# A two-layer diffusion trunk on one core: the first parameter loads regrouped, a weight strip cut differently, one rounding step moved between engines, and a new planned order

## The chip, the core and the metric

The kernel runs on one NeuronCore of a Trainium2 chip. Its engines are TensorE (PE in the profile, its weight loads PEld), VectorE (DVE), ScalarE (ACT), GpSimd (POOL) and SyncE (SP), which issues most DMAs; ScalarE can issue DMAs as well (ACTq). The metric is the time of one execution in microseconds (us) of device time; lower is better.

## The reference

Two layers work on 256 latent tokens and 256 context tokens, each of 1024 numbers in float32. A layer computes six modulation vectors from a conditioning vector, `silu(c) @ w_mod + b_mod`, normalises and modulates the tokens, multiplies them by an input matrix of 1024 x 3096, runs three groups of mixing heads on the result, multiplies by an output matrix, and adds that to the tokens. A mixture of 32 experts (each token takes two) follows. In short:

```python
mod = split(silu(c) @ w_mod[l] + b_mod[l], 6)
h   = (rmsnorm(x, norm1_w[l]) * (1 + mod[1]) + mod[0]) @ w_in[l]      # 3096 columns
m   = concat(diff_attention(h), ssm_mixer(h), gdn_mixer(h))          # three head groups
x   = x + mod[2] * (m @ w_out[l])
x   = x + mod[5] * hier_moe(modulate(rmsnorm(x, norm2_w[l]), mod[3], mod[4]))
```

In the 3096 columns of `w_in`, columns 2048 to 2055 are `dt`, the eight step sizes of the state-space heads; columns 2056 to 2311 are `q`, 2312 to 2567 `k` and 2568 to 2823 `v` of the delta-rule heads; columns 2824 to 3095 are that group's gate with 16 rate columns.

## The kernel before

The program is written as a list of operations (`Prog.record`), which a planner then puts in order (`Prog._schedule`). The planner keeps a clock for each engine and takes, again and again, the operation that could start first; among equals the one of highest priority. A priority is the cost of what still hangs on an operation, plus a bias by label (`CFG`, such as `"inQ"` or `"OUT2"`), plus random noise of a given size and seed (`ORDER`: one tuple of run length, noise, seed and warm gap for each of three parts of the program). Each engine executes its own list strictly in the planned order. SP's DMAs keep the order in which the code names them. Where the planner expects TensorE to be idle for longer than the warm gap it fills the gap with idle products (L536). All memory is one arena that the planner hands out; loaded weights share a ring of limited size, so a load can wait until an older weight has been used.

The planner's costs are a model. A mark with `after=n` keeps the operations under it from being planned before the first n of the list (DMAs of SP aside) are all planned.

The beginning of layer 0, the stretch that the diff touches, works so:

- SP loads `c`, constants, the four token tiles (512 KB each, `xtok`), then `wm0`, the eight 1 MB chunks of `w_mod` that give the first two modulation vectors (L971), then the first four strips of `w_in` (`first_loads`, L1063), and so on.
- ScalarE's queue issues 28 small parameter loads (the list `small`, L953 to L973): row vectors of both layers into the tiles `ra`, `row` and `rb`. After `csil` it also issues the two loads `wdt` (L984): eight columns of `w_in` for each layer, 1024 runs of 32 bytes each.
- TensorE transposes the token tiles; ScalarE and VectorE copy them out to `xT`; ScalarE squares them (L1005), `inverse` makes the reciprocal norm, and VectorE makes the products `v0` (L1009), eight of 128x512.
- `modulation` (L874) multiplies the eight `w_mod` chunks and adds `b_mod`; `mod_cols` makes the columns of scale and shift.
- For each of eight feature blocks k (L1099 on), `h` is wanted in two parts: `hhi`, rounded to float32r, and `hlo`, the remainder. With `v0`, ScalarE writes `hhi` directly (two ACTIVATEs of 128x256), VectorE makes the same value unrounded as `u` (two TENSOR_SCALARs of 128x256), and VectorE (even k) or GpSimd (odd k) subtracts.
- `tokm(0, ...)` (L1218) is the first projection: strip 0 (272 columns) and `wdt` (8 columns) are split into a rounded part and a remainder by `split` (L1046), and each of four token tiles takes 24 products of 280 columns. Its results start the chain "rates". Then `feat` projects k (strip 1), v (strip 2) and q (strip 3).
- `param_prep` (L1015) turns the small parameters into columns and broadcasts; it is the first thing recorded after the token part, ahead of `mixers`.

Later stretches, which only the new order touches: the rest of layer 0's mixers, to about 560 us; layer 0's experts; layer 1's mixers; layer 1's experts.

Of the kernel before, what the change touches and what calls it, by code (L numbers as in the profile page):

```python
# [9 lines left out]
F32 = mybir.dt.float32  # L10
# [102 lines left out]
TICK, WARM = 3413.3, 2800.0  # L113
# [661 lines left out]
def trunk(tc, pg, A, out, xd, dbg, layers, stop):  # L775
# [43 lines left out]
    def transpose(o, i):  # L819
        pe.transpose(o, i, ident[:i.shape[0], :i.shape[0]])  # L820
# [47 lines left out]
    ra = [T([104, P], name="ra") for _ in range(2)]  # L868
# [82 lines left out]
    wdt = T([P, 2, KC, 8], name="wdt", stays=True)  # L951
    gp.memset(row, 0.0)
    small = []  # L953
    for l in range(2):
        small += [(ra[l][0:48, :], A["b_mod"][l].rearrange("(r p) -> r p", p=P)),
                  (ra[l][48:56, :], A["norm1_w"][l].rearrange("(r p) -> r p", p=P)),
                  (ra[l][56:64, :], A["norm2_w"][l].rearrange("(r p) -> r p", p=P)),
                  (ra[l][64:70, :], A["ssm_conv_b"][l].rearrange("(r p) -> r p", p=P)),
                  (ra[l][70:100, :], A["ssm_conv_w"][l].rearrange("t (i p) -> (t i) p", p=P)),
                  (ra[l][100:104, :], A["ssm_norm_w"][l].rearrange("(r p) -> r p", p=P))]  # L960
    for o, nm, n in ((0, "ssm_dt_bias", 16), (16, "gdn_dt_bias", 8), (32, "ssm_a_log", 16), (48, "gdn_a_log", 8),
                     (56, "ssm_d", 8), (64, "router_g_b", 4), (68, "router_e_b", 32), (104, "diff_lq1", 32),
                     (136, "diff_lq2", 32), (168, "diff_lk1", 32), (200, "diff_lk2", 32)):
        ap = A[nm]
        small.append((row[:, :, o:o + n], bass.AP(tensor=ap.tensor, offset=ap.offset, ap=[[0, 1], [n, 2], [1, n]])))
    small.append((rb[0:60, :], A["gdn_conv_w"].rearrange("l t (i p) -> (l t i) p", p=P)))
    for o, nm, n in ((60, "diff_norm_w", 64), (62, "gdn_norm_w", 64), (64, "diff_qn_w", 32), (66, "diff_kn_w", 32)):
        ap = A[nm]
        small.append((rb[o:o + 2, :].rearrange("p (h q) -> p h q", q=n),
                      bass.AP(tensor=ap.tensor, offset=ap.offset, ap=[[n, 2], [0, P // n], [1, n]])))  # L970
    wm0 = [mod_load(l0, 0, k) for k in range(KC)]  # L971
    for dst, src in small:
        ac.dma_start(dst, src)  # L973
# [8 lines left out]
                     cs.rearrange("p (s k) -> p s k", s=2), OP.mult)  # L982
    for l in range(2):
        ac.dma_start(wdt[:, l], A["w_in"][l].rearrange("(k p) n -> p k n", p=P)[:, :, 2048:2056], wait=[csil])  # L984

    def row_prep(l):
        pt = ps("pt")
        transpose(pt[:, 0:104], ra[l])
        ve.tensor_copy(prm[l][:, 0:64], pt[:, 0:64])
        ve.tensor_scalar(prm[l][:, 64:104], pt[:, 64:104], 0.5, None, OP.mult)  # L990

    row_prep(0)
# [22 lines left out]
    def param_prep():  # L1015
        ve.tensor_copy(identb, ident)
        for n_, nm in zip(negm, ("le", "ge")):
            ve.tensor_scalar(n_, c(nm), 1.0, 1e30, OP.subtract, OP.mult)
        row_prep(1)
        o = ps("pbc")  # L1020
        mm(o[:, 0:464], c("ones")[0:1].to_broadcast([1, P]), row.rearrange("p l x -> p (l x)"))
        ve.tensor_copy(bcs.rearrange("p l x -> p (l x)"), o[:, 0:464])
        pt = ps("pt")
        transpose(pt[:, 0:68], rb)
        ve.tensor_scalar(pb[:, 0:60], pt[:, 0:60], 0.5, None, OP.mult)
        ve.tensor_copy(pb[:, 66:68], pt[:, 66:68])
        ve.tensor_scalar(pb[:, 62:64], pt[:, 62:64], 0.5, None, OP.mult)
        ve.tensor_scalar(pb[:, 64:66], pt[:, 64:66], 32 ** -0.5, None, OP.mult)
        for l in range(2):
            li = 0.8 - 0.6 * math.exp(-0.3 * l)  # L1030
            ve.tensor_scalar(pb[:, 60 + l:61 + l], pt[:, 60 + l:61 + l], 1.0 - li, None, OP.mult)
# [31 lines left out]
    def first_loads(l):  # L1063
# [3 lines left out]
        pieces += [W[:, :, a:a + 256] for a in (2312, 2568, 2056,  # L1067
# [5 lines left out]
        for i, p_ in enumerate(pieces[:4]):  # L1073
            ws.append(wload(p_, 8, 256 if i else 272, "w"))
            if i == 1 and l == layers[0]:
                cast_consts()
        return pieces, ws, {(1, 0): split(ws[1], 0, P, CFG[l]["parts"])} if CFG[l]["early"] else {}


    def mixers(l, wm=None, v0=None):  # L1080
# [18 lines left out]
        for k in range(KC):  # L1099
            u = T([P, TOK], name="hk")  # L1100
            for s in range(2):
                sl = slice(256 * s, 256 * s + 256)
                sc, bi = cols(s, k)
                if v0:
                    ac.activation(hhi[k][:, sl], v0[k][:, sl], AF.Identity, scale=sc, bias=bi)
                    ve.tensor_scalar(u[:, sl], v0[k][:, sl], sc, bi, OP.mult, OP.add)
# [7 lines left out]
            if k % 2 and not v0:  # L1114
                ac.copy(hhi[k], u)
            if k % 2 or v0:
                (gp if k % 2 else ve).tensor_tensor(hlo[k], u, hhi[k].bitcast(F32), OP.subtract)
# [67 lines left out]

        pieces, ws, early = first_loads(l)
        WZ, WS = 7, 9
# [30 lines left out]
        tokm(0, 272, 256, got, wdt[:, l])  # L1218
# [102 lines left out]
        for i in range(2):  # L1321
            o = feat(1, P * i)
# [5 lines left out]
        for i in range(2):  # L1328
            o = feat(2, P * i)
# [3 lines left out]
        for i in range(2):  # L1333
            o = feat(3, P * i, lo)
# [815 lines left out]
    mark("params")  # L2150
    param_prep()
    for l in layers:
# [13 lines left out]
ORDER = [(2500.0, 1500.0, 994, 900.0), (2500.0, 100.0, 270, 600.0), (0.0, 500.0, 79, 2000.0)]  # L2166
# [3 lines left out]
    {"rings": 26624, "ring0": 6, "gdn": 5e+05, "inS": 0, "inZ": 1e+05, "SSM": 1e+05, "inQ": 4.29e+05, "inV": 2e+05,  # L2170
     "ATT": 1e+05, "mod": 0, "OUT": 47800, "OUT2": 50000, "route": 1e+05, "ring": 2.5, "units": 3, "proj": 2, "gate":
     1, "lssm": 2, "latt": 3, "early": 1, "ahead": 11, "loop": 0, "nowait": -1, "mroute": 0, "mpos": 14, "modr":
     1e+06, "parts": 2, "margin": (8, 16, 0)},
    {"rings": 28672, "ring0": 6, "gdn": 1e+06, "inS": 7.15e+05, "inZ": 2e+06, "SSM": 50000, "inQ": 50000, "inV":
     12400, "ATT": 1e+06, "mod": 0, "OUT": 50000, "OUT2": 0, "route": 4e+06, "ring": 2, "units": 3, "proj": 4, "gate":
     1, "lssm": 2, "latt": 2, "early": 1, "ahead": 9, "loop": 0, "nowait": -1, "mroute": 3, "mpos": 9, "modr": 6e+05,
     "parts": 2, "margin": (16, 8, 1)}]
# [23 lines left out]
```

## Time and profile before

| what | value |
|---|---|
| median of 3 runs | 1909.54 us (1909.12 to 1909.98) |
| the profiled execution, its own time | 1907.57 us |
| its span in the profile | 1905.8 us |
| busy share of PE, DVE, ACT, POOL | 93%, 47%, 28%, 21% |
| mean granted TensorE clock | 0.971 of full speed |
| moved by DMA | 503.41 MB, 264 GB/s over the span |

The span runs from the first to the last instruction; 1.8 us of the execution's own time lie around it. Busy shares are averages over stages with different limits. A granted clock of 1.00 is 2.4 GHz and of 0.50 is 1.2 GHz; a stretch between them is a mixture in time. In a row that ends in `[1.36 <-DVE arena_r L352]`, the engine sat idle for 1.36 us before that instruction and VectorE ended the wait. Nearly every instruction carries line L352, that of the helper that records it, so shapes tell the rows apart.

### The profile page before, as it was taken

Reading aid. Unit: us, or ns where it says so; the run is one execution under the profiler, and the core shown is the slowest. Engines: PE = TensorE matmul, PEld = TensorE weight load, DVE = VectorE, ACT = ScalarE, POOL = GpSimd, SP = SyncE. Lnnn points to the kernel's source line nnn. Section 1 sums busy time; section 2 is a strip of 40 time slices with the busy share of each in tenths; the row PEclk is TensorE's granted clock in tenths of the full one; section 3 lists DMA queues with packets and bytes.
Section 4 is the critical chain, followed back from the end, with each engine's and each line's share of the span. In section 5 each row is a group of like instructions: output and inputs, shape, how many; then the busy total and the mean of one; then the engine's idle time right before and its main releaser. Section 6 shows DMA issues by size and latency. Waiting matters only on the chain. (4 is left out here: it accounts for less than half of the span.)

```text
span 1905.8 us, 34790 instructions
## 1 busy us (share of the span) xinstructions
PE 1781.1 (93%) x13912; PEld 1266.5 (66%) x13912; DVE 891.4 (47%) x2440; ACT 542.6 (28%) x1432; POOL 403.4 (21%) x649
## 2 busy tenths in 40 slices
PE   5889999989989999999999999999899999999998
PEld 2767786657975656657565878877686655566654
DVE  3785556855531433333234885766751323222222
ACT  2466444533310101111011466564321111011101
POOL 0254453474100000000000346652910000000000
PEclk8898989998989999999999999999899999999999
DMA  8510006373159999899999520106929999999997
GB/s 301 196 45 26 21 2 220 113 263 128 63 196 371 421 420 421 334 390 421 376 422 385 172 79 20 46 24 243 339 93 361 421 420 421 421 421 420 421 421 289
DMA packets 108272, 503.41 MB, mean 264 GB/s; under 512 B 14893, under 2 KB 39753, under 8 KB 53833
## 3 DMA queue, kind: packets, MB, share of 16 engines
q1 hardware_dynamic: 105552, 500.91, 66.5%
q8 instruction: 112, 1.84, 0.4%
q10 hardware_dynamic: 2553, 0.21, 0.1%
q14 instruction: 55, 0.45, 0.1%
HBM read 495.85 MB, written 5.24 MB: 263 GB/s over the span
## 5 line engine op out<-in xcount | busy, mean ns | idle before, releaser
L352 PE MATMUL psum<-arena 128*64 128x256 f32 (+14 forms) x9808 | 1190.4, 369 | 99.0 <-DVE arena L352 38.2
L352 PEld LDWEIGHTS psum<-arena 128*64 128x64 f32 (+3 forms) x9784 | 734.2, 147 | 521.5 <-issue 219.0
L352 PE MATMUL psum<-arena_r 128*128 128x256 f32 (+3 forms) x3336 | 604.2, 330 | 20.7 <-ACT arena_r L352 6.5
L352 PEld LDWEIGHTS psum<-arena_r 128*128 128x128 f32 x3336 | 486.4, 195 | 107.1 <-issue 36.7
L352 POOL TENSOR_TENSOR arena<-arena 128x128 f32<-128x128 f32 (+4 forms) x500 | 272.5, 568 | 275.9 <-DVE arena L352 142.9
L352 DVE SCALAR_TENSOR_TENSOR arena<-psum,arena 128x256 f32<-128x256 f32 (+4 forms) x649 | 271.3, 473 | 94.8 <-PE psum L352 81.1
L352 ACT COPY arena<-psum 64x128 f32<-64x128 f32 (+3 forms) x524 | 176.9, 358 | 458.0 <-PE psum L352 371.2
L352 DVE SCALAR_TENSOR_TENSOR arena<-arena,psum 128x256 f32<-128x256 f32 (+1 forms) x194 | 84.6, 442 | 407.9 <-PE psum L352 208.2
L352 POOL TENSOR_TENSOR arena_r<-arena,arena_r 128x512 fp32r<-128x512 f32 (+3 forms) x55 | 78.1, 1426 | 639.9 <-PE psum L352 500.7
L352 DVE TENSOR_TENSOR arena<-arena,psum 64x128 f32<-64x128 f32 (+4 forms) x384 | 116.3, 320 | 116.1 <-PE psum L352 65.5
L352 ACT ACTIVATE arena<-psum 128x256 f32<-128x256 f32 (+2 forms) x103 | 37.3, 366 | 360.6 <-PE psum L352 347.0
L352 DVE SCALAR_TENSOR_TENSOR arena_r<-psum,arena,arena_r 128x512 fp32r<-128x512 f32 x64 | 47.5, 748 | 175.0 <-ACT arena_r L352 174.5
L352 ACT ACTIVATE arena<-arena 128x256 f32<-128x256 f32 (+8 forms) x204 | 85.2, 445 | 138.3 <-DVE arena L352 107.5
L352 ACT ACTIVATE arena_r<-psum,arena 128x512 fp32r<-128x512 f32 x64 | 43.9, 687 | 247.7 <-PE psum L352 247.5
L352 ACT ACTIVATE arena<-psum,arena 128x128 f32<-128x128 f32 (+2 forms) x216 | 88.2, 464 | 75.7 <-PE psum L352 58.9
L352 DVE COPY arena<-psum 128x512 f32<-128x512 f32 (+10 forms) x117 | 39.8, 350 | 125.9 <-PE psum L352 113.7
L352 ACT CAST arena_r<-arena 128x512 fp32r<-128x512 f32 (+3 forms) x140 | 83.3, 635 | 41.4 <-PE psum L352 27.0
L352 DVE TENSOR_TENSOR arena_r<-arena,arena_r 128x512 fp32r<-128x512 f32 (+4 forms) x93 | 80.1, 877 | 21.1 <-ACT arena_r L352 20.3
L352 DVE SCALAR_TENSOR_TENSOR arena<-arena 128x4 f32<-128x4 f32 (+6 forms) x264 | 78.0, 308 | 10.9 <-POOL arena L352 5.5
L352 DVE TENSOR_TENSOR arena<-arena 128x4 f32<-128x4 f32 (+9 forms) x234 | 75.3, 341 | 10.1 <-ACT arena L352 6.9
L352 DVE TENSOR_SCALAR arena<-arena 128x4 int32<-128x4 int32 (+16 forms) x162 | 45.6, 301 | 14.7 <-DMA arena<-in_consts_dram 8.6
L536 PE MATMUL psum<-arena 128*128 128x128 f32 x384 | 49.0, 283 | 0.0
(31 smaller groups left out, 306.0 us busy)
## 6 DMA issues: line engine op xcount, KB each, us to landing
arena<-in_exp_w_gate_dram SPq DMA_DIRECT2D x128, 1024.0 KB, 19.8
arena<-in_exp_w_up_dram SPq DMA_DIRECT2D x128, 1024.0 KB, 12.5
arena<-in_exp_w_down_dram SPq DMA_DIRECT2D x120, 1024.0 KB, 17.0
arena<-in_w_mod_dram SPq DMA_DIRECT2D x48, 1024.0 KB, 5.3
arena<-in_w_in_dram SPq DMA_DIRECT2D x22, 1024.0 KB, 9.4
arena<-in_exp_w_down_dram SPq DMA_DIRECT2D x16, 512.0 KB, 17.2
xd<-arena SPq DMA_DIRECT2D x16, 256.0 KB, 4.7
arena<-xd SPq DMA_DIRECT2D x16, 256.0 KB, 5.3
```

What stands on the lines that cost most here:

```text
L352: inst(*[self.real(a) for a in args], **{k: self.real(a) for k, a in kw.items()})
L536: self.nc.tensor.matmul(o, one, one, start=True, stop=True, skip_group_check=True)
```

## The change

It has five parts.

1. The early parameter loads on ScalarE's queue shrink from 28 to three (`b_mod`, `norm1_w`, `norm2_w`, each for both layers at once). The others, 20 loads now, go to SP's queue as `small_loads`, named after strip 1 of `w_in` and ahead of strip 2.
2. `wdt` is gone. `dt` and q come in one strip of 264 columns, loaded as the second strip; k and v follow as third and fourth. The first projection takes its `dt` from that strip, and q is projected from its columns 8 on.
3. `prm` is filled in two steps: the modulation's columns early, the rest in `param_prep`, which is now recorded within `mixers` under a mark with `after=n0`, so that it is planned once all of `h` is.
4. In the first norm, ScalarE writes `u` (float32), VectorE copies it to `hhi` and makes all eight subtractions; GpSimd makes none there.
5. `ORDER` and `CFG` have other values, and the planner counts TensorE as warm from 3000 instead of 2800 on.

```diff
-TICK, WARM = 3413.3, 2800.0
+TICK, WARM = 3413.3, 3000.0
...
-    for l in range(2):
-        small += [(ra[l][0:48, :], A["b_mod"][l].rearrange("(r p) -> r p", p=P)),
...
-    for dst, src in small:
-        ac.dma_start(dst, src)
+    for r0, r1, ap in ((0, 48, A["b_mod"].rearrange("l (r p) -> r l p", p=P)),
+                       (48, 56, A["norm1_w"].rearrange("l (r p) -> r l p", p=P)),
+                       (56, 64, A["norm2_w"].rearrange("l (r p) -> r l p", p=P))):
+        ac.dma_start(ra[r0:r1], ap)
     wm0 = [mod_load(l0, 0, k) for k in range(KC)]
+    def small_loads():
+        for r0, r1, ap in ((64, 70, A["ssm_conv_b"].rearrange("l (r p) -> r l p", p=P)),
+                           (100, 104, A["ssm_norm_w"].rearrange("l (r p) -> r l p", p=P))):
+            sy.dma_start(ra[r0:r1], ap)
+        for l in range(2):
+            sy.dma_start(ra[70:100, l, :], A["ssm_conv_w"][l].rearrange("t (i p) -> (t i) p", p=P))
+        for o, nm, n in ((0, "ssm_dt_bias", 16), (16, "gdn_dt_bias", 8), (32, "ssm_a_log", 16), (48, "gdn_a_log", 8),
+                         (56, "ssm_d", 8), (64, "router_g_b", 4), (68, "router_e_b", 32), (104, "diff_lq1", 32),
+                         (136, "diff_lq2", 32), (168, "diff_lk1", 32), (200, "diff_lk2", 32)):
+            ap = A[nm]
+            sy.dma_start(row[:, :, o:o + n], bass.AP(tensor=ap.tensor, offset=ap.offset, ap=[[0, 1], [n, 2], [1, n]]))
+        sy.dma_start(rb[0:60, :], A["gdn_conv_w"].rearrange("l t (i p) -> (l t i) p", p=P))
+        for o, nm, n in ((60, "diff_norm_w", 64), (62, "gdn_norm_w", 64), (64, "diff_qn_w", 32), (66, "diff_kn_w", 32)):
+            ap = A[nm]
+            sy.dma_start(rb[o:o + 2, :].rearrange("p (h q) -> p h q", q=n),
+                         bass.AP(tensor=ap.tensor, offset=ap.offset, ap=[[n, 2], [0, P // n], [1, n]]))
...
-        ac.dma_start(wdt[:, l], A["w_in"][l].rearrange("(k p) n -> p k n", p=P)[:, :, 2048:2056], wait=[csil])
...
         pieces = [W[:, :, 2824:3096]]
-        pieces += [W[:, :, a:a + 256] for a in (2312, 2568, 2056,
+        pieces += [W[:, :, 2048:2312]]
+        pieces += [W[:, :, a:a + 256] for a in (2312, 2568,
...
             if i == 1 and l == layers[0]:
+                small_loads()
+            if i == 2 and l == layers[0]:
                 cast_consts()
...
                 if v0:
-                    ac.activation(hhi[k][:, sl], v0[k][:, sl], AF.Identity, scale=sc, bias=bi)
-                    ve.tensor_scalar(u[:, sl], v0[k][:, sl], sc, bi, OP.mult, OP.add)
+                    ac.activation(u[:, sl], v0[k][:, sl], AF.Identity, scale=sc, bias=bi)
...
-            if k % 2 and not v0:
-                ac.copy(hhi[k], u)
             if k % 2 or v0:
-                (gp if k % 2 else ve).tensor_tensor(hlo[k], u, hhi[k].bitcast(F32), OP.subtract)
+                (ve.tensor_copy if v0 else ac.copy)(hhi[k], u)
+                (ve if v0 else gp).tensor_tensor(hlo[k], u, hhi[k].bitcast(F32), OP.subtract)
...
+        n0 = len(pg.ops)
         pieces, ws, early = first_loads(l)
+        if v0:
+            mark("params", after=n0)
+            param_prep()
+            mark("norm")
...
-        tokm(0, 272, 256, got, wdt[:, l])
+        tokm(0, 272, 256, got, ws[1][:, :, 0:8])
...
-            o = feat(3, P * i, lo)
+            o = feat(1, 8 + P * i, lo)
...
-ORDER = [(2500.0, 1500.0, 994, 900.0), (2500.0, 100.0, 270, 600.0), (0.0, 500.0, 79, 2000.0)]
+ORDER = [(2500.0, 1500.0, 298, 2000.0), (2500.0, 100.0, 42, 900.0), (0.0, 1000.0, 754, 900.0)]
```

In `CFG` of layer 0, `inZ` goes from 1e5 to 1.79e5, `inQ` from 4.29e5 to 1e6, `inV` from 2e5 to 1e5, `ATT` from 1e5 to 1.1e5, `mod` from 0 to 4540, `OUT` from 47800 to 50200, and `nowait` from -1 to 0 (strip 0 may now be split before `hhi[0]` is there). In that of layer 1, `inQ` goes from 50000 to 42800, `inV` from 12400 to 16700, `OUT2` from 0 to 1e6 and `route` from 4e6 to 1.86e7.

## Rows read from the trace of the kernel before

**Rows 1.** Busy time by windows: us, engines' busy time, clock, DMA share, GB/s.
```profile
core 0: us, PE busy (x) PEld busy (x) DVE busy (x) ACT busy (x) POOL busy (x), PEclk, DMA share, GB/s
0.00:10.00 10.00, 2.13 (x9) 1.66 (x10) 0.94 (x6) 1.47 (x2) 0.91 (x6) 1.00 0.64 191
...
17.50:20.00 2.50, 2.38 (x21) 0.69 (x13) 1.49 (x8) 0.87 (x4) 0.44 (x3) 1.00 0.16 26
...
25.00:27.50 2.50, 1.79 (x9) 0.49 (x2) 0.00 (x0) 0.00 (x0) 0.00 (x0) 0.50 1.02 424
27.50:30.00 2.50, 2.50 (x10) 0.35 (x12) 1.22 (x6) 0.28 (x2) 0.35 (x3) 0.50 0.63 182
30.00:32.50 2.50, 1.88 (x12) 0.20 (x4) 0.95 (x6) 1.15 (x4) 0.00 (x0) 0.72 0.69 197
...
42.50:45.00 2.50, 0.94 (x9) 0.70 (x7) 1.96 (x7) 0.48 (x2) 0.00 (x0) 1.00 1.12 361
```

**Rows 2.** Waits of SP's own queue, first 60 us: total, times, longest.
```profile
SPq L352 <- DMA arena<-in_w_in_dram: 21.6, 4, 9.8
```

**Rows 3.** Timeline of SP and ACT: start, length, what, [idle before].
```profile
7.92 23.04 SPq L352 DMA_DIRECT2D arena<-in_w_mod_dram  x8
...
9.64 0.41 ACTq L352 DMA_DIRECT2D arena<-in_w_in_dram  x1
...
15.28 0.57 ACTq L352 DMA_DIRECT2D arena<-in_gdn_a_log_dram  x1
...
21.74 0.45 ACTq L352 DMA_DIRECT2D arena<-in_w_in_dram  x1
...
31.92 1.06 ACT L352 ACTIVATE arena<-arena 128x1024 f32<-128x1024 f32 x1 [1.07 <-PE psum L352]
...
44.60 1.09 ACT L352 ACTIVATE arena_r<-arena 128x256 fp32r<-128x256 f32 x2 [2.02 <-DVE arena L352]
```

**Rows 4.** Timeline of PE and DVE, 40 to 74 us.
```profile
40.12 3.31 PE L352 MATMUL psum<-arena 128*32 128x512 f32 x20 [0.44 <-DMA arena<-in_w_mod_dram]
...
46.85 0.40 PE L352 MATMUL psum<-arena_r 128*128 128x280 f32 x1 [3.41 <-ACT arena_r L352]
...
65.61 8.80 PE L352 MATMUL psum<-arena_r 128*128 128x280 f32 x57 [1.36 <-DVE arena_r L352]
...
72.70 0.18 DVE L352 COPY arena<-psum 128x24 f32<-128x24 f32 x1
```

**Rows 5.** Groups by shape, DVE, 40 to 66 us: busy us, mean ns, idle.
```profile
L352 DVE TENSOR_TENSOR arena_r<-arena,arena_r 128x512 fp32r<-128x512 f32 x6 | 7.7, 1304 | 0.0
L352 DVE TENSOR_SCALAR arena<-arena 128x256 f32<-128x256 f32 x16 | 6.8, 468 | 0.9 <-POOL arena_r L352 0.7
L352 DVE TENSOR_TENSOR arena<-arena,psum 128x512 f32<-128x512 f32 x8 | 5.4, 681 | 2.8 <-PE psum L352 2.6
L352 DVE TENSOR_TENSOR arena_r<-arena,arena_r 128x1088 fp32r<-128x1088 f32 x1 | 1.3, 1278 | 0.0
L352 DVE CAST arena<-arena 128x1024 bf16<-128x1024 f32 x1 | 0.7, 676 | 0.0
```

**Rows 6.** Groups by shape, ACT, 40 to 66 us.
```profile
L352 ACT ACTIVATE arena_r<-arena 128x256 fp32r<-128x256 f32 x16 | 8.4, 591 | 8.2 <-DVE arena L352 8.2
L352 ACT CAST arena_r<-arena 128x1088 fp32r<-128x1088 f32 x2 | 2.2, 1088 | 0.0
```

**Rows 7.** Groups by shape, PE, 46 to 74 us.
```profile
L352 PE MATMUL psum<-arena_r 128*128 128x280 f32 x96 | 15.4, 317 | 9.9 <-DVE arena_r L352 4.1 <-ACT arena_r L352 3.4 <-POOL arena_r L352 2.3
```

**Rows 8.** Busy time by windows, the later stages.
```profile
100.00:150.00 50.00, 46.63 (x421) 35.96 (x419) 40.76 (x109) 30.69 (x88) 23.12 (x35) 1.00 0.13 43
...
80.00:600.00 520.00, 481.13 (x3978) 380.48 (x3978) 305.63 (x920) 222.56 (x640) 205.07 (x345) 0.93 0.34 120
600.00:1050.00 450.00, 439.25 (x3195) 278.83 (x3191) 161.16 (x377) 49.31 (x102) 0.48 (x1) 1.00 0.98 399
```

**Rows 9.** Idle products (L536) alone, 80 to 600 us.
```profile
80.00:600.00 520.00, 7.83 (x60) 7.17 (x60) 0.93 0.34 120
```

More of the change, by code (lines that the diff above doesn't have):

```diff
@@ L867, in trunk @@
     csil = T([P, KC, 32], name="csil", stays=True)
-    ra = [T([104, P], name="ra") for _ in range(2)]
+    ra = T([104, 2, P], name="ra")
     prm = [T([P, 104], name=f"prm{l}", stays=True) for l in range(2)]
@@ L950, in trunk @@
     row = T([1, 2, 232], name="row")
-    wdt = T([P, 2, KC, 8], name="wdt", stays=True)
     gp.memset(row, 0.0)
-    small = []
-    for l in range(2):
-        small += [(ra[l][0:48, :], A["b_mod"][l].rearrange("(r p) -> r p", p=P)),
[L956 to L970, printed above, removed]
-    wm0 = [mod_load(l0, 0, k) for k in range(KC)]
-    for dst, src in small:
-        ac.dma_start(dst, src)
+    for r0, r1, ap in ((0, 48, A["b_mod"].rearrange("l (r p) -> r l p", p=P)),
+                       (48, 56, A["norm1_w"].rearrange("l (r p) -> r l p", p=P)),
+                       (56, 64, A["norm2_w"].rearrange("l (r p) -> r l p", p=P))):
+        ac.dma_start(ra[r0:r1], ap)
@@ L982, in trunk @@
                      cs.rearrange("p (s k) -> p s k", s=2), OP.mult)
+    pt = ps("pt")
     for l in range(2):
-        ac.dma_start(wdt[:, l], A["w_in"][l].rearrange("(k p) n -> p k n", p=P)[:, :, 2048:2056], wait=[csil])
[L986 to L992, printed above, removed]
+        transpose(pt[:, 64 * l:64 * l + 64], ra[0:64, l, :])
+        ve.tensor_copy(prm[l][:, 0:64], pt[:, 64 * l:64 * l + 64])
     xx = T([P, KC, TOK], name="xT")
@@ L1018, in param_prep @@
             ve.tensor_scalar(n_, c(nm), 1.0, 1e30, OP.subtract, OP.mult)
-        row_prep(1)
+        for l in range(2):
+            pt = ps("pt")
+            transpose(pt[:, 0:104], ra[:, l, :])
+            ve.tensor_scalar(prm[l][:, 64:104], pt[:, 64:104], 0.5, None, OP.mult)
         o = ps("pbc")
@@ L1073, in first_loads @@
         for i, p_ in enumerate(pieces[:4]):
-            ws.append(wload(p_, 8, 256 if i else 272, "w"))
+            ws.append(wload(p_, 8, (272, 264, 256, 256)[i], "w"))
             if i == 1 and l == layers[0]:
+                small_loads()
+            if i == 2 and l == layers[0]:
                 cast_consts()
-        return pieces, ws, {(1, 0): split(ws[1], 0, P, CFG[l]["parts"])} if CFG[l]["early"] else {}
+        return pieces, ws, {(2, 0): split(ws[2], 0, P, CFG[l]["parts"])} if CFG[l]["early"] else {}
     def mixers(l, wm=None, v0=None):
@@ L1321, in mixers @@
         for i in range(2):
-            o = feat(1, P * i)
+            o = feat(2, P * i)
             conv(o, gk[i], gw(2 + i), 0.0)
@@ L1328, in mixers @@
         for i in range(2):
-            o = feat(2, P * i)
+            o = feat(3, P * i)
             vt = T([P, TOK], name="cv")
@@ L2148, in output @@
                 sy.dma_start(out[0, P * t:P * t + P, 512 * h:512 * h + 512], y)
-    mark("params")
-    param_prep()
     for l in layers:
@@ L2169 @@
 CFG = [
[L2170 to L2177, printed above, removed]
+    {"rings": 26624, "ring0": 6, "gdn": 5e+05, "inS": 0, "inZ": 1.79e+05, "SSM": 1e+05, "inQ": 1e+06, "inV": 1e+05,
+     "ATT": 1.1e+05, "mod": 4540, "OUT": 50200, "OUT2": 50000, "route": 1e+05, "ring": 2.5, "units": 3, "proj": 2,
+     "gate": 1, "lssm": 2, "latt": 3, "early": 1, "ahead": 11, "loop": 0, "nowait": 0, "mroute": 0, "mpos": 14,
+     "modr": 1e+06, "parts": 2, "margin": (8, 16, 0)},
+    {"rings": 28672, "ring0": 6, "gdn": 1e+06, "inS": 7.15e+05, "inZ": 2e+06, "SSM": 50000, "inQ": 42800, "inV":
+     16700, "ATT": 1e+06, "mod": 0, "OUT": 50000, "OUT2": 1e+06, "route": 1.86e+07, "ring": 2, "units": 3, "proj": 4,
+     "gate": 1, "lssm": 2, "latt": 2, "early": 1, "ahead": 9, "loop": 0, "nowait": -1, "mroute": 3, "mpos": 9, "modr":
+     6e+05, "parts": 2, "margin": (16, 8, 1)}]
 _INS = ['x', 'c', 'ctx', 'c_ctx', 'w_mod', 'b_mod', 'norm1_w', 'norm2_w', 'w_in', 'w_out', 'diff_qn_w', 'diff_kn_w',
```

## The prediction

> **What bounds the kernel now.** I read the windows first. From 600 to 1050 us, the first experts, DMA is busy 0.98 at 399 GB/s and PE 439 of 450 us: weights stream at full rate and PE barely keeps up. From 80 to 600 us PE is busy 481 of 520 us while DMA is busy 0.34, and 0.13 from 100 to 150 us [rows 8]. So the mixers are bound by PE and what it waits for, and the experts by their stream, which waits for memory that the mixers free. Neither has a date of its own: if the mixers begin earlier, the rest moves along. The last layer is built the same.
>
> The beginning is different. In its first 70 us neither holds. The rows to see: DMA moves 26 GB/s at 17.5 to 20 us, 182 and 197 GB/s at 27.5 to 32.5 us, against 424 GB/s just before the second hole [rows 1]. SP is at that time handing out the `w_mod` chunks, from 7.92 to 30.96 us [rows 3]. What it waited for is the `w_in` loads, 21.6 us in four waits, the longest 9.8 us [rows 2]; before 31 us the only `w_in` loads are the two `wdt`, issued on ScalarE's queue at 9.64 and 21.74 us [rows 3]. A wait of SP's queue for a load of ScalarE's queue, with no data between the two, is what leaves the DMA engines empty. The last `w_mod` chunk is used at 40.12 us [rows 4], the first modulated block starts at 44.60 us [rows 3], TensorE's last wait for `hlo` or a split strip ends at 65.61 us, and the last result of the first projection is copied out at 72.70 us [rows 4]. These four times are the scale for what follows.
>
> **The change part by part.**
>
> *Early loads and `wdt`.* Until the last `w_mod` chunk, DMA must move 0.43 MB of constants, 2.1 MB of tokens and 8.39 MB of `w_mod`, by the shapes 10.9 MB. With no holes, at 424 GB/s [rows 1], that is 25.7 us; the first 10 us moved only 1.9 MB [rows 1]. If they go as before, the other 9.0 MB end at 31.2 us; if the rate is full from 2.5 us on, at 28.2 us. I take 30 us for the use of the last chunk, against 40.12: **10 us earlier**. From the other side: the holes alone, 2.5 us at 26 and 5 us at 190 instead of 424 GB/s, are worth 2.3 + 2.8 = 5.1 us. From there to the first modulated block I leave the 4.5 us of before (40.12 to 44.60): 34.5 us.
>
> ScalarE loses some 25 DMA issues, up to 0.57 us each [rows 3], and the waits among them. Its four squares, which began at 31.92 us [rows 3] although the tokens had landed long before, can run by 20 us, and so the eight products `v0` on DVE, 5.4 us [rows 5], which lay between the blocks of `h`, come before the modulation.
>
> *The tokens.* On ScalarE nothing changes in number: 16 ACTIVATEs, 8.4 us, and 2.2 us for strip 0's casts [rows 6], with the narrower strips some 12 us. On DVE the 16 TENSOR_SCALARs (6.8 us) go. Eight copies of 128x512 come: the trace has none of this form; half of the 1024-wide CAST is 0.34 us, a two-input operation of that width 0.68 us [rows 5]; I take 0.4, since it too has one input, 3.2 us in all. Four more subtractions come from GpSimd, so eight at 0.68 us are 5.4 us; before, six of that kind had a mean of 1.30 us [rows 5]. With strip 0's share of 1.3 us and small ones DVE has some 10 us, at most 13. DVE and ScalarE work side by side: `h` and the split strip take some 13 us after the first block instead of 21.0 (44.60 to 65.61): ready at 47.5, **18 us earlier**.
>
> *Strip with `dt`.* The first product now needs strips 0 and 1, 2.2 MB, at 361 GB/s 6 us [rows 1]: 36 us, before most of `h`. The first projection's 96 products take 15.4 us of PE [rows 7]; PE was at half clock in part of that time before, when it stood waiting for `h` [rows 1, 7]. Starting at 37 us and with 3 us for a slow clock at the start it ends at 56 us, now bound by PE itself, against 72.70: **16 us earlier**. Bounds: 53 us with no slow clock (20 us), 62 us if it can start only at 46 (10 us). The 128-word `wdt` tile and its two splits become a view of strip 1: nothing either way. In layer 1 `dt` is likewise in the second strip, loaded ahead in the shadow of the last experts; I price that at 0, and at up to 3 us, one strip's transfer, if that cover is gone. Strip 1 stays in the ring until q is projected, which holds back loads used tens of us later: 0.
>
> *The 20 loads on SP.* One such load took 0.57 us to issue on ScalarE's queue [rows 3]; the eleven into `row` at that, and the nine others at half of it by estimate, take 9 us of SP's time. Behind them stand strip 2 (k), the constants, strip 3 (v) and the stores of `xT`. Strip 2 then lands at about 36 + 9 + 3 = 48 us; PE wants it when the first projection ends, 56 us. Covered by 8 us; without cover at most 9 us. Behind the parameters wait `param_prep`'s operations on PE and DVE, but the mark puts them after the last block of `h`, at 47.5 us, when the last loads land: 0 to 3 us, which the 3 us for PE's slow start may hide.
>
> The Trainium skill (DMA: Bandwidth & Descriptors, Issuing engines are not separate DMA queues) says that DMAs of several engines share the same 16 DMA engines, and that issuing from several saves only the sequencers' issue time. By it, moving 20 loads onto SP buys nothing and gives back that saving; taken strictly it would also make ScalarE's loads nearly free to SP before, and the trace disagrees, with 9.8 us of one wait.
>
> *The new order.* It moves every later stage by an amount that no row gives. What it can win or lose lies between 80 and 600 us: PE idles 520 - 481 = 39 us there, and a mean clock of 0.93 is worth 0.07 x 520 = 36 us [rows 8]. A new drawing of noise and biases I put at 0, give or take 8 us, about a tenth of the two together. The wider warm gap drops some of the 60 idle products [rows 9], too few to matter.
>
> Sum: 1907.57 us (the profiled execution's own time) less 16 is 1891.6; that execution lies 2.0 us under the median, so **1893.5 us**.
>
> **The rivals.**
>
> *SP's queue becomes the brake* (12 in 100). If the 20 issues hold the parameters and strip 2 back beyond 50 us, or planned operations on PE queue up behind the parameters ahead of the first projection, that projection starts at 46 and ends at 62 us: 10 us won, 1899.5. For it: TensorE and DVE execute in planned order, and the planner reckons each SP issue at 50 ns. Against it: the mark `after=n0`. It is the case that the Trainium skill's rule on issuing engines (DMA: Bandwidth & Descriptors) points to.
>
> *The order is better as well* (10 in 100): half-clock and idle time between 80 and 600 us falls by a tenth to a fifth more, 12 us: 1881.
>
> *The gain stays at the beginning* (7 in 100): later stages wait for something with a date of its own, and the end does not move: 1908. Against it speaks DMA's idleness from 100 us on [rows 8].
>
> *Slower* (11 in 100): the new order with its wide warm gap leaves gaps in which the clock falls. It decides once the loss to half clock grows from 36 to over 52 us, 16 more. If it grows by two thirds, 24 us, the time is 1917. Against it: only 7.8 us of idle products stood between 80 and 600 us [rows 9], so little was held up by them.
>
> **How the numbers follow.** The forecast has 60 in 100, with its own range of 1885 to 1902: 16 us with bounds of 10 and 20, and 8 for the order, not all of them at once. Measurements of this kernel tell 0.2%, 3.8 us, from no change. Faster: 60 + 12 + 10 and 2 of the third rival, 84 in 100; same 5; slower 11. The range for 8 in 10 reaches from 1881, the better order, to 1908, where the gain is lost, and leaves out the slower case and half of the better one.
>
> **What would show it.** In the profile after: no hole in DMA before 36 us; SP's waits for `w_in` gone; the last `w_mod` chunk used at about 30 us; the first modulated block at 34 to 35, the first projection's end at 53 to 58 us; GpSimd without subtractions for `h`; at 600 us and at the end the same distance of some 16 us. I am wrong in the sum if the distance at 75 us is under 8 us; wrong about the passage if it is 16 there and gone at 1050 us; wrong about the order if it changes by over 8 us between 80 and 600 us.

## The result: 1890.6 us, 1.0% less, and the time forecast came out for partly other reasons

The changed kernel takes 1890.62 us (median of 6 runs, 1886.13 to 1898.01) beside 1909.76 us for the kernel before (6 runs, 1908.64 to 1916.01): a ratio of 0.9899, 95% interval 0.9876 to 0.9923. The forecast was 1893.5 us, with a range of 1881 to 1908. The profiled execution took 1890.12 us, its span 1888.3 us.

I read the same views as before, in the same order. First the windows of the beginning of the changed kernel (columns as in [rows 1]):

```profile
17.50:20.00 2.50, 1.27 (x9) 0.29 (x9) 0.23 (x1) 2.40 (x6) 0.00 (x0) 0.98 1.01 419
...
25.00:27.50 2.50, 2.50 (x16) 1.58 (x15) 0.76 (x2) 0.00 (x0) 0.00 (x0) 0.66 1.01 419
27.50:30.00 2.50, 1.28 (x12) 0.16 (x8) 2.50 (x5) 0.00 (x0) 0.00 (x0) 1.00 1.00 397
...
37.50:40.00 2.50, 0.91 (x2) 0.66 (x3) 2.43 (x5) 1.81 (x4) 0.90 (x1) 0.50 0.00 0
40.00:42.50 2.50, 2.50 (x12) 2.50 (x12) 2.33 (x5) 1.09 (x2) 0.00 (x0) 0.50 0.00 0
42.50:45.00 2.50, 2.22 (x13) 1.99 (x11) 0.40 (x1) 0.00 (x0) 0.00 (x0) 0.75 0.05 14
```

The holes of [rows 1] are gone: 419 GB/s where 26 stood, 397 where 182 stood. A new hole has come, from 37.5 to 45 us, in which DMA moves next to nothing. The waits of SP's own queue in the first 60 us (total, times, longest) agree with the first half; 21.6 us of [rows 2] have become 5.6. Before 31 us, while SP hands out the `w_mod` chunks, its waits for `w_in` go from 18.7 us in two to none. The 5.6 us all come after that, where the kernel before waited for 2.9:

```profile
SPq L352 <- DMA arena<-in_w_in_dram: 5.6, 4, 2.4
```

The timeline of SP and ScalarE shows what lies in the new hole:

```profile
3.89 6.76 SPq L352 DMA_DIRECT2D arena<-in_w_mod_dram  x8
...
16.43 1.06 ACT L352 ACTIVATE arena<-arena 128x1024 f32<-128x1024 f32 x1 [0.32 <-PE psum L352]
...
26.77 3.56 SPq L352 DMA_DIRECT2D arena<-in_ssm_conv_b_dram  x1
...
35.74 1.73 ACT L352 ACTIVATE arena<-arena 128x256 f32<-128x256 f32 x3
...
40.62 1.09 ACT L352 ACTIVATE arena<-arena 128x256 f32<-128x256 f32 x2 [1.08 <-DVE arena_r L352]
...
43.86 0.26 SPq L352 DMA_DIRECT2D arena<-in_diff_kn_w_dram  x1
...
44.24 0.40 SPq L352 DMA_DIRECT2D arena<-in_w_in_dram  x1
...
49.70 1.14 ACT L352 CAST arena_r<-arena 128x512 fp32r<-128x512 f32 x2 [7.99 <-DMA arena<-in_w_in_dram]
50.74 4.05 ACT L352 ACTIVATE arena<-arena 128x256 f32<-128x256 f32 x8
```

The `w_mod` chunks are handed out in 6.76 us (before 23.04, [rows 3]), the squares begin at 16.43 us (31.92) and the first modulated block at 35.74 us (44.60). But from 26.77 to 44.12 us SP hands out the 20 small loads, and strip 2 goes out only behind them, at 44.24 us. ScalarE's planned list has the split of strip 2, the two CASTs, in the middle of `h`, after eight of its 16 ACTIVATEs. ScalarE stands for 7.99 us until strip 2 has landed, and the other eight ACTIVATEs come behind it. On PE and DVE (timeline, as in [rows 4]) this looks so:

```profile
31.74 1.06 PE L352 MATMUL psum<-arena 128*32 128x512 f32 x8 [2.94 <-DMA arena<-in_w_mod_dram]
...
38.83 0.57 PE L352 MATMUL psum<-arena_r 128*128 128x280 f32 x1 [4.21 <-DVE arena_r L352]
...
50.87 1.29 DVE L352 TENSOR_TENSOR arena_r<-arena,arena_r 128x512 fp32r<-128x512 f32 x2 [7.97 <-DMA arena<-in_consts_dram]
...
52.55 0.83 PE L352 MATMUL psum<-arena_r 128*128 128x280 f32 x2 [7.84 <-DVE arena_r L352]
...
68.64 0.18 DVE L352 COPY arena<-psum 128x24 f32<-128x24 f32 x1
```

The last `w_mod` chunk is used at 31.74 us instead of 40.12, the first product of the first projection comes at 38.83 instead of 46.85, and then PE and DVE stand 8 us, too. (DVE's row is its part of the split, which needs ScalarE's CASTs; the view names the constants as releaser, since they land at about the same time. An experiment below tells the two apart.) The last copy comes at 68.64 instead of 72.70 us: 4.1 us earlier, where I had forecast 16.

The prices of the moved work, by groups (DVE from 35 to 58 us, ScalarE from 10 to 60 us, PE from 0 to 70 us), answer to [rows 5 to 7]:

```profile
L352 DVE TENSOR_TENSOR arena_r<-arena,arena_r 128x512 fp32r<-128x512 f32 x10 | 6.7, 687 | 8.1 <-DMA arena<-in_consts_dram 8.0
L352 DVE CAST arena_r<-arena 128x512 fp32r<-128x512 f32 x8 | 4.7, 593 | 1.8 <-ACT arena L352 1.7
...
L352 ACT ACTIVATE arena<-arena 128x256 f32<-128x256 f32 x16 | 8.5, 594 | 1.2 <-DVE arena_r L352 1.1
...
L352 PE MATMUL psum<-arena_r 128*128 128x280 f32 x96 | 17.5, 349 | 12.7 <-DVE arena_r L352 12.7
```

And the windows of the later stages, which answer to [rows 8], with two stretches more:

```profile
0.00:600.00 600.00, 538.02 (x4309) 414.97 (x4310) 351.10 (x1038) 251.60 (x710) 212.00 (x360) 0.94 0.42 153
...
80.00:600.00 520.00, 485.91 (x4035) 377.52 (x4035) 314.48 (x942) 222.57 (x648) 205.04 (x347) 0.95 0.37 136
600.00:1050.00 450.00, 443.75 (x3233) 294.43 (x3232) 176.80 (x422) 55.09 (x113) 3.41 (x4) 0.99 0.97 393
...
600.00:640.00 40.00, 39.55 (x269) 23.14 (x269) 19.85 (x48) 4.44 (x10) 0.00 (x0) 1.00 1.01 421
```

A lead is how much earlier the changed kernel comes to the same point than the kernel before. By 600 us DMA has moved 600 x 153 GB/s = 91.8 MB. The same window of the kernel before reads 141 GB/s, 84.6 MB. From there on the experts' weights stream at full rate, 421 GB/s, so 7.2 MB more by 600 us are, by this estimate, 17 us of lead. Measured so, the lead is made in two pieces, 4 us at 70 us and another 13 between there and 600 us, and is 17.5 us at the end (1905.8 to 1888.3 us of span). At points of the program it grows and shrinks: 9.3 us where the first overflow loop of the experts is entered, the loop for experts with more tokens than their places hold (546.2 to 536.9), 25.2 at the first product of layer 1 (1074.2 to 1049.1), 18.3 where the second overflow loop is entered (1426.5 to 1408.3).

### The profile page after: what moved, and what is told of

The parts are those of the page before. It is cut to its first block, busy times and chain, and to the rows that moved or that the text cites. A ratio compares the mean times of both kernels' runs of the same rounds, so it can differ in the third digit from the quotient of the medians.

```text
span 1888.3 us, 34616 instructions
## 1 busy us (share of the span) xinstructions
PE 1766.9 (94%) x13852; PEld 1253.8 (66%) x13852; DVE 899.3 (48%) x2436; ACT 542.5 (29%) x1432; POOL 397.3 (21%) x645
## 3 DMA queue, kind: packets, MB, share of 16 engines
q8 instruction: 111, 1.82, 0.4%
## 5 line engine op out<-in xcount | busy, mean ns | idle before, releaser
L352 PE MATMUL psum<-arena 128*64 128x256 f32 (+12 forms) x9810 | 1184.2, 367 | 95.8 <-DVE arena L352 33.4
L352 PE MATMUL psum<-arena_r 128*128 128x256 f32 (+3 forms) x3336 | 594.4, 329 | 20.0 <-DVE arena_r L352 15.5
L352 POOL TENSOR_TENSOR arena<-arena 128x128 f32<-128x128 f32 (+5 forms) x500 | 275.0, 575 | 281.5 <-DVE arena L352 196.6
L352 POOL TENSOR_TENSOR arena_r<-arena,arena_r 128x512 fp32r<-128x512 f32 (+3 forms) x51 | 71.1, 1401 | 640.4 <-ACT arena_r L352 633.2
L352 ACT ACTIVATE arena<-arena 128x256 f32<-128x256 f32 (+7 forms) x220 | 92.6, 457 | 131.0 <-DVE arena L352 94.9
L352 DVE COPY arena<-psum 128x512 f32<-128x512 f32 (+12 forms) x117 | 40.3, 350 | 120.2 <-PE psum L352 99.6
L352 DVE TENSOR_TENSOR arena_r<-arena,arena_r 128x512 fp32r<-128x512 f32 (+3 forms) x97 | 85.3, 897 | 25.0 <-ACT arena_r L352 16.6
L352 DVE TENSOR_TENSOR arena<-arena 128x4 f32<-128x4 f32 (+7 forms) x234 | 76.6, 341 | 17.9 <-ACT arena L352 14.8
L352 DVE TENSOR_SCALAR arena<-arena 128x4 int32<-128x4 int32 (+14 forms) x146 | 38.1, 270 | 9.1 <-ACT arena L352 6.4
L536 PE MATMUL psum<-arena 128*128 128x128 f32 x322 | 42.3, 289 | 0.0
```

The costliest lines, as they stand in the source:

```text
L352: inst(*[self.real(a) for a in args], **{k: self.real(a) for k, a in kw.items()})
L536: self.nc.tensor.matmul(o, one, one, start=True, stop=True, skip_group_check=True)
```

## The experiments

All were compared with the kernel before on the same chip. For each the table gives the median, the ratio with its interval, and from one profile the last copy of the first projection, the entry of the first overflow loop, the first product of layer 1 (us), and what DMA moved on the average from 0 to 600 us. Two profiles of the same kernel differ by up to 5 us at the end, as the two pairs of spans show (1888.3 and 1890.8 us, 1884.2 and 1879.2). The runs were made on several chips, on which the kernel before took 1909.0 to 1912.2 us, so a difference between two rows of the table is uncertain by some 3 us more than one within a row.

| kernel | median, us | ratio to before | last copy | overflow 1 | layer 1 | GB/s to 600 |
|---|---|---|---|---|---|---|
| before | 1909.0 to 1912.2 | 1 | 72.70 | 546.2 | 1074.2 | 141 |
| changed | 1890.62 | 0.9899 (0.9876 to 0.9923) | 68.64 | 536.9 | 1049.1 | 153 |
| changed, second time | 1891.34 | 0.9895 (0.9872 to 0.9918) | 68.15 | 539.5 | 1051.5 | 151 |
| new order alone | 1914.58 | 1.0016 (0.9998 to 1.0034) | 69.29 | 555.2 | 1072.2 | 138 |
| new beginning, old settings, seed 1 | 1978.18 | 1.0358 (1.0318 to 1.0397) | 70.34 | 581.0 | 1112.9 | 122 |
| before, `wdt` in one run | 1911.47 | 0.9996 (0.9977 to 1.0016) | 70.12 | 542.1 | 1072.6 | 144 |
| changed, small loads behind strip 3 | 1883.71 | 0.9853 (0.9824 to 0.9883) | 58.95 | 529.3 | 1041.0 | 158 |
| the same, second time | 1883.42 | 0.9870 (0.9848 to 0.9891) | 58.78 | 529.2 | 1040.6 | 159 |
| changed, small loads behind strip 2 | 1891.00 | 0.9905 (0.9884 to 0.9925) | 66.78 | 538.5 | 1047.8 | 152 |
| changed, 20 more small loads | 1907.48 | 0.9982 (0.9963 to 1.0000) | 80.55 | 551.8 | 1063.0 | 143 |
| changed, old second part | 1927.05 | 1.0068 (1.0038 to 1.0099) | 69.35 | 541.3 | 1063.4 | 148 |
| changed, second part with seed 2 | 1910.85 | 1.0001 (0.9977 to 1.0025) | 69.14 | 536.5 | 1052.2 | 153 |
| changed, first part with seed 1 | 1963.15 | 1.0271 (1.0235 to 1.0308) | 68.86 | 565.2 | 1104.4 | 129 |

### The order alone

The kernel before with the new `ORDER`, `CFG` and `WARM`.

```
-TICK, WARM = 3413.3, 2800.0
+TICK, WARM = 3413.3, 3000.0
-ORDER = [(2500.0, 1500.0, 994, 900.0), (2500.0, 100.0, 270, 600.0), (0.0, 500.0, 79, 2000.0)]
+ORDER = [(2500.0, 1500.0, 298, 2000.0), (2500.0, 100.0, 42, 900.0), (0.0, 1000.0, 754, 900.0)]
(and both entries of CFG as in the change)
```

> The kernel before with the new values of ORDER, CFG and WARM, and nothing else of the change. Theory 1 (the beginning brings the time, the order nothing): 1909.5 us, give or take 8. Theory 2 (read from the two traces: 4 us of the distance are there at the end of the first projection, the rest comes later): 1896 us, 13 us less than before.

Measured: 1914.58 us, not faster. On the old list of operations the new settings win nothing. In parts they act both ways: the last copy of the first projection comes at 69.29 us, 3.4 us earlier than before, nearly as early as in the changed kernel; the first overflow loop is entered 9.0 us later than before, at 555.2 us; and the stretch from there to layer 1 takes 517.1 instead of 528.0 us.

### The beginning alone

The changed kernel with the settings of the kernel before. With their first seed (994) the planner finds no plan for the new list of operations that fits in memory, so the first drawing has seed 1.

```
-ORDER = [(2500.0, 1500.0, 298, 2000.0), (2500.0, 100.0, 42, 900.0), (0.0, 1000.0, 754, 900.0)]
+ORDER = [(2500.0, 1500.0, 1, 900.0), (2500.0, 100.0, 270, 600.0), (0.0, 500.0, 79, 2000.0)]
(and CFG, WARM as before the change)
```

> The changed kernel with ORDER, CFG and WARM of before, but seed 1 in place of 994 in the first part (with 994 the planner finds no room). Theory 1 (the beginning brings the time): 1893 us, give or take 8 for the other draw. Theory 2 (the beginning brings 4 us): 1905 us, give or take 8. The first projection's end is read from the trace: 56 us by the forecast, 68 where ScalarE's planned order waits for strip 2.

Measured: 1978.18 us, 67 us slower than the kernel before on the same chip, although its first projection ends 2.4 us earlier than there. So the beginning can't be had "alone": the noise is drawn one number after another along the list of operations, so an operation more or less moves all that follows, and a drawing with an arbitrary seed cost more than the whole change is worth.

### The hole in DMA: `wdt` in one run

The kernel before, its plan unaltered; the `wdt` tile is read as 128 runs of 256 bytes instead of 1024 of 32. It leaves out the right step sizes: they come from other numbers of `w_in`.

```
-        ac.dma_start(wdt[:, l], A["w_in"][l].rearrange("(k p) n -> p k n", p=P)[:, :, 2048:2056], wait=[csil])
+        ac.dma_start(wdt[:, l], A["w_in"][l, 0:P, 2048:2112].rearrange("p (k n) -> p k n", k=KC), wait=[csil])
```

> The kernel before with each wdt load reading 128 runs of 256 bytes in place of 1024 runs of 32 bytes, so that the step sizes come from other numbers of w_in; every planned order stays as it was. If SP's waits on these two loads make the holes in DMA, the last w_mod chunk is used at 33 to 35 us instead of 40.1, the first projection ends 5 to 7 us earlier, and, if a gain at the beginning passes to the end, the time is 1903 us. If the holes have another cause, all stays: 1909.5. If later stages take the gain back, the first projection ends earlier and the time is 1908 to 1910.

Measured: 1911.47 us, no change. Its windows, columns as in [rows 1]:

```profile
17.50:20.00 2.50, 1.16 (x10) 0.16 (x8) 1.85 (x14) 0.27 (x1) 0.44 (x3) 1.00 0.84 301
25.00:27.50 2.50, 2.50 (x10) 0.40 (x12) 1.11 (x5) 0.22 (x1) 0.35 (x3) 0.50 0.71 184
27.50:30.00 2.50, 2.33 (x12) 0.20 (x4) 1.05 (x8) 0.77 (x4) 0.00 (x0) 0.50 0.96 392
```

And the waits of its SP queue in the first 60 us, with SP's row for the `w_mod` chunks:

```profile
SPq L352 <- DMA arena<-in_w_in_dram: 13.6, 4, 6.9
SPq L352 <- DMA arena<-in_b_mod_dram: 4.2, 2, 3.7
SPq L352 <- DMA arena<-in_ssm_conv_w_dram: 2.5, 1, 2.5
SPq L352 <- DMA arena<-in_diff_lk_dram: 2.5, 1, 2.5
SPq L352 <- DMA arena<-in_diff_lq_dram: 1.9, 1, 1.9
...
7.84 23.39 SPq L352 DMA_DIRECT2D arena<-in_w_mod_dram  x8
```

Where 26 GB/s stood, 301 stand, and 392 for 182; but from 25 to 27.5 us 184 stand for 424. The short runs made part of the holes, and part has moved. SP's waits for `w_in` fall from 21.6 to 13.6 us, but SP is not freer for it: what these waits lost, waits for other loads of ScalarE's queue gained (for all loads of that queue, in the first 31 us, 22.3 us in the kernel before and 22.4 here), and SP hands out the `w_mod` chunks in 23.39 us instead of 23.04. So SP's waits hang on the loads of that queue as a whole; longer runs in two of them don't change the total. The last `w_mod` chunk is used 3.6 us earlier all the same (36.52 us), the first projection ends 2.6 us earlier, and at layer 1 1.6 us of it are left. At the end no gain can be measured, but the interval, 3 to 4 us either way, can't exclude one of 2.6 us.

### The small loads behind strip 3

The changed kernel, its plan unaltered. The main part of the edit is shown: when the planner comes to the 20 small loads, they are kept and written into SP's list after the next four DMAs (strip 2, the two constants, strip 3).

```
+            if o.label == "small":
+                held.append(o)
+            elif held and (e != "SP" or len(passed) == 4) and (len(passed) == 4 or any(h in o.deps for h in held)):
+                for h in held:
+                    self._emit(h)
+                held = []
+            if o.label != "small":
+                self._emit(o)
+                if held and e == "SP":
+                    passed.append(o)
```

> The changed kernel with its 20 small loads issued by SP after strip 3 instead of ahead of strip 2; the planned order of all other engines and every address stay. Theory: ScalarE's planned order has the split of strip 2 ahead of the last eight ACTIVATEs of h, and strip 2 comes late because of the 20 issues, so ScalarE stands still from 42 to 50 us. Then the still stand goes, the first projection ends at 60 to 61 us instead of 68.6, and the time is 1883 us (7 us less than the changed kernel). Rival: the parameters become the brake, PE or DVE wait for them instead, and the time stays at 1890.

Measured: 1883.71 us. The timeline of ScalarE and DVE:

```profile
40.54 1.09 ACT L352 ACTIVATE arena<-arena 128x256 f32<-128x256 f32 x2 [1.02 <-DVE arena_r L352]
41.54 1.13 ACT L352 CAST arena_r<-arena 128x512 fp32r<-128x512 f32 x2
42.57 4.04 ACT L352 ACTIVATE arena<-arena 128x256 f32<-128x256 f32 x8
...
47.89 0.69 DVE L352 TENSOR_TENSOR arena_r<-arena,arena_r 128x512 fp32r<-128x512 f32 x1
...
58.95 0.18 DVE L352 COPY arena<-psum 128x24 f32<-128x24 f32 x1
```

The stand before the CASTs is gone, the other eight ACTIVATEs begin at 42.57 instead of 50.74 us, and the first projection ends at 58.95 us, 13.75 us earlier than before the change. I timed it once more, beside the changed kernel itself:

> The changed kernel with the small loads put behind strip 3, timed once more, in more rounds, beside the changed kernel itself. Theory (the 9.7 us that this wins at the first projection reach the end in part): 4 to 8 us faster than the changed kernel. Rival (they are lost on the way, as the 2.6 us that the wdt in one run won): within 2 us of it.

> The changed kernel itself, unaltered, as the measure for the two others: 1889 to 1892 us.

Measured: 1883.42 and 1891.34 us. Of the 9.4 us won at the first projection (68.15 to 58.78) 7.9 reach the end by the medians; by the means of these five and six runs it is 6.1 us, give or take some 5. With the first timing the direction is clear: this version is faster than both kernels.

### Only behind strip 2

The same with one DMA let past instead of four, so that the constants stay behind the small loads.

```
-            elif held and (e != "SP" or len(passed) == 4) and (len(passed) == 4 or any(h in o.deps for h in held)):
+            elif held and (e != "SP" or len(passed) == 1) and (len(passed) == 1 or any(h in o.deps for h in held)):
```

> The changed kernel, its planned order unaltered, with the 20 small loads put behind strip 2 but still ahead of the constants and strip 3 on SP. Theory A (ScalarE's split of strip 2 was the one thing that the small loads held up): as with the loads put behind strip 3, the first projection's last copy at 59 us, time 1884. Theory B (what they hold up is whatever SP issues behind them that is planned into the middle of h; DVE's cast of the constants stands there too, between the copies): ScalarE goes on at 41, DVE stands before the cast of the constants until about 50, the last copy comes at 66 to 69 us, time 1888 to 1892.

Measured: 1891.00 us, last copy at 66.78 us: theory B. The timeline of ScalarE and DVE:

```profile
41.33 1.12 ACT L352 CAST arena_r<-arena 128x512 fp32r<-128x512 f32 x2
42.36 3.05 ACT L352 ACTIVATE arena<-arena 128x256 f32<-128x256 f32 x6
...
50.68 0.17 DVE L352 CAST arena_r<-arena 64x24 fp32r<-64x24 f32 x1 [6.53 <-DMA arena<-in_consts_dram]
...
50.88 1.09 ACT L352 ACTIVATE arena<-arena 128x256 f32<-128x256 f32 x2 [5.47 <-DVE arena_r L352]
```

ScalarE passes the split of strip 2 without a wait, and then DVE stands before the cast of the constants, which the plan has put between its copies for `h`. In the changed kernel this second stand lies hidden behind the first.

### Twenty more small loads

The changed kernel, its plan unaltered, with 20 DMAs of 256 bytes more on SP ahead of strip 2, into memory that nobody reads. The lines that issue them:

```
+        for i in range(20):
+            pg.ops[-1].fns.append(lambda i=i: nc.sync.dma_start(pg.junk[i:i + 1, :], A["norm1_w"][0:1, 64 * (i % 8):64 * (i % 8) + 64]))
```

> The changed kernel, its planned order unaltered, with 20 more small loads of 256 bytes issued on SP ahead of the split strip 2 (they land in memory that nobody reads). At 0.4 us each SP hands out strip 2 some 8 us later. Theory (ScalarE stands before the split of strip 2, so each us of SP's queue is a us of the beginning, and part of it reaches the end, as with the loads moved behind, 9.6 us earlier there and 4 to 7 at the end): the first projection's last copy at 76 to 77 us, time 1894 to 1898. Rival 1 (it passes on in full): 1899. Rival 2 (later waits take it up): 1891, within 1.5.

Measured: 1907.48 us, above all that I had expected. The rows of SP's timeline that matter:

```profile
30.52 16.35 SPq L965 DMA_DIRECT2D junk<-in_norm_w_dram  x20
...
56.60 0.40 SPq L352 DMA_DIRECT2D arena<-in_w_in_dram  x1
```

The dose was half as large again as I had reckoned: of the 16.35 us 3.5 are waits for `w_in`, and a load took 0.59 us (the median), not 0.4. Strip 2 goes out 12.4 us later and the last copy comes at 80.55 us, 11.9 us later than in the first profile of the change. The end moves by 16 to 17 us by the medians, by 13 to 17 when each kernel is set against the kernel before on its own chip. So a delay here passes on in full; whether it grows on the way is not shown. And this kernel, whose first projection ends 7.9 us *later* than before the change, is still not slower than the kernel before. What it wins, it wins behind the first projection.

### Other drawings

Three kernels that keep the changed program, and of which each alters one drawing: the second part's settings as before the change; the second part with seed 2; the first part with seed 1.

```
-ORDER = [(2500.0, 1500.0, 298, 2000.0), (2500.0, 100.0, 42, 900.0), (0.0, 1000.0, 754, 900.0)]
+ORDER = [(2500.0, 1500.0, 298, 2000.0), (2500.0, 100.0, 270, 600.0), (0.0, 1000.0, 754, 900.0)]
(and the second entry of CFG as before the change)
```
```
+ORDER = [(2500.0, 1500.0, 298, 2000.0), (2500.0, 100.0, 2, 900.0), (0.0, 1000.0, 754, 900.0)]
```
```
+ORDER = [(2500.0, 1500.0, 1, 2000.0), (2500.0, 100.0, 42, 900.0), (0.0, 1000.0, 754, 900.0)]
```

> The changed kernel with the second drawing (noise, seed, warm gap) and the second layer's biases of the kernel before; the beginning and the first mixers keep their new order. Theory (the new drawing of this part carries most of the 17 us): the stretch from the first overflow point to the first product of layer 1, 512 us after the change and 528 before, goes back to about 528, layer 1's mixers give back 5, and the time is 1901 us (1896 to 1906). Rival (the earlier beginning carries it, the drawing is worth nothing either way): 1891 us, within 3.

> The changed kernel with one number altered: the second drawing's seed is 2 instead of 42, so the noise on the priorities of the first experts and layer 1's mixers is another sample of the same size. Theory (a drawing is worth tens of us): this part takes 884 to 907 us instead of 873.5, the time is 1901 to 1925 us. Rival (the prediction's term, 0 give or take 8 us): 1883 to 1899 us.

> The changed kernel with the first drawing's seed 1 instead of 298: another sample of the noise on the priorities of the beginning and the first mixers. Theory (a drawing is worth tens of us): the first overflow point comes 10 to 45 us later than at 537, the time is 1900 to 1935 us. Rival (0 give or take 8 us): 1883 to 1899 us.

Measured: 1927.05, 1910.85 and 1963.15 us, that is some 35, 20 and 70 us more than the changed kernel. The old second part lies far above the 1901 that I expected, and for another reason: the stretch from the overflow loop to layer 1 takes 522 us, not 528, and layer 1's mixers don't give back 5 us but lose another 28 (387.3 us from the first product of layer 1 to the second overflow loop, against 359.2; the profiled execution was the slowest of the six, 8 us over their median). A setting that was good for one list of operations isn't for another. With seed 1 in the first part DMA has moved 129 GB/s on the average by 600 us instead of 153, and TensorE, from 80 to 600 us, was busy for 469 us at a mean clock of 0.92 instead of 486 at 0.95:

```profile
80.00:600.00 520.00, 468.96 (x3850) 372.72 (x3850) 299.75 (x924) 222.21 (x636) 203.97 (x345) 0.92 0.30 108
```

## Why the prediction was right, and where its steps failed

The time was right because two terms were wrong by nearly the same amount in opposite directions. By the signs that the prediction named, the sum at the beginning is refuted (the distance at 75 us is 4, under 8), and so is the term for the order (by the bytes moved the distance changes by 13 between 80 and 600 us, more than 8; at the first overflow loop it had grown by only 5, at layer 1 by 21).

*Early loads and `wdt`: right.* 30 us was forecast for the use of the last `w_mod` chunk, 31.74 was measured; 34.5 for the first block, 35.74 measured; the holes went, and so did SP's waits for `w_in` before 31 us. The prediction put all 21.6 us of these waits to the two `wdt` loads; 2.9 us of them come after 31 us and are for strips. That loads on ScalarE's queue hold up SP's is borne out, but by the queue as a whole: with `wdt` in few runs other loads of that queue held SP up as long, and only with `wdt` and 25 of the 28 small loads gone did the `w_mod` chunks go out in 6.76 us. Why SP waits for them, with no data between, no run here shows.

*The tokens: right in its prices, not in its result.* A clean copy took 0.42 us (forecast 0.4), a subtraction on DVE 0.69 (0.68), and the 16 ACTIVATEs 8.5 us (8.4). The first copy took 1.82 us, at the same time as GpSimd's subtraction for the split, which brings the mean to 0.593. `h` would have been ready near 48 us, as forecast (47.5): with the small loads out of the way the last ACTIVATE ends at 46.6 us and the last subtraction at 48.6. In the changed kernel it was not, because of the next step.

*The 20 loads on SP: the step that failed.* "Strip 2 then lands at about 48 us; PE wants it when the first projection ends, 56 us. Covered by 8 us." The landing was about right: its wait ended at 49.7 us. The loads occupied SP for 17.35 us (26.77 to 44.12), of which 5.6 were waits, rather than 9, but SP also reached them earlier than I had reckoned. Wrong was who wants strip 2. I looked for the product that uses it, and overlooked that its split stands in ScalarE's list in the middle of `h`, and the cast of the constants in DVE's. An engine that executes a planned order waits for data at the place of the plan, not at the place of need. The two experiments on SP's order show both waits, and price the step: 9.4 to 9.7 us at the first projection, by the medians 7 to 8 at the end.

Had this not been, the first projection would have ended 13.75 us earlier instead of 16, within the bounds of 10 and 20 and 3 us later than the 56 forecast. So the rival "SP's queue becomes the brake" named the right queue and what it holds back, strip 2. Its path and its price were off: it let the first projection start at 46 us, and in fact this started at 38.83 and stood still in the middle; it left 10 us won, and 4.1 were. The Trainium skill's rule that DMAs issued from several engines share the same 16 DMA engines and save only the sequencer's time (DMA: Bandwidth & Descriptors, Issuing engines are not separate DMA queues) is borne out here in what it implies for this move, that the loads cost SP its time to issue them: 11.75 us without the waits, and 9.4 to 9.7 us were won at the first projection when they no longer stood in the way.

*The passage: right.* A delay at the beginning reaches the end: with the last copy at 58.8, 68.2 and 80.6 us the kernel takes 1883.4, 1891.3 and 1907.5 us, 24 us over 21.8 (the last on another chip). In the kernel before with `wdt` in one run, 2.6 us at the first projection can't be found again at the end; they are too few for the noise to tell whether they were lost.

*The new order: wrongly sized.* I put the redrawing at 0, give or take 8 us. Between two points on that line, the last copy at 72.70 us as before the change would give 1891.3 + (72.70 - 68.15) x (16.1 / 12.4) = 1897 us. By this estimate some 6 of the 19 us come from the beginning and 13 from what the plan does after it. Nor are the 4 us at the beginning shown to be the edits' own, since the new settings on the old list bring the last copy to 69.29 us, too. Between 80 and 600 us PE idles 34 instead of 39 us, and the loss to half clock is 0.05 x 520 = 26 instead of 36: together 15 us less, a fifth of the two, where I had allowed for a tenth. (Busy time counts idle products, too, and these fell from 7.8 to 2.8 us.) Three other drawings show the size that the term can have: some 20 to 70 us, and all to the worse. My 8 us would have been far too narrow for settings taken at random.

*What stays open.* Whether the 13 us belong to the new settings or to the new list of operations can't be told: the settings on the old list bring nothing, the old settings on the new list don't fit, or with another first seed cost 67 us, and no setting that was tried is good for both. Nor did I separate the narrower strips, the later parameters and the tokens from one another within the beginning, since each alters the list and so redraws the order.

## What to carry to other kernels

Where engines execute a planned order, ask of every load that becomes later which instruction on *any* engine stands first in line for it, preparation work like a cast or a split included, and what is queued behind that. A change to the list of a planned program redraws the plan, here worth more than the change itself, so tell the two apart with edits that leave the plan as it is. And check a right time against its milestones: it can be the sum of two wrong terms.

## What the runs showed that I had not expected

- SP's twenty small loads took 17.35 us in the changed kernel, with 5.6 us of waits; twenty of 256 bytes from memory to memory took 16.35 us, with 3.5 us of waits. That is 0.59 us each in the first case and 0.64 in the second. I had reckoned with 0.4 to 0.45 on the average.
- With the `wdt` tile in 1024 runs of 32 bytes DMA moved 26 GB/s in the window from 17.5 to 20 us [rows 1]; with 128 runs of 256 bytes, and nothing else altered, 301. SP's waits for the loads of ScalarE's queue stayed as long in total, 22 us.
- A copy of 128x512 on DVE took 0.42 us alone, and 1.82 us while GpSimd subtracted. The rows of the kernel with the small loads behind strip 3, where it is the same:

```profile
35.83 2.50 POOL L352 TENSOR_TENSOR arena_r<-arena,arena_r 128x1088 fp32r<-128x1088 f32 x1 [18.87 <-ACT arena_r L352]
36.78 1.83 DVE L352 CAST arena_r<-arena 128x512 fp32r<-128x512 f32 x1 [1.75 <-ACT arena L352]
...
39.36 0.42 DVE L352 CAST arena_r<-arena 128x512 fp32r<-128x512 f32 x1
```
